# One of forty loads moved to another queue: the second load issued by ScalarE while SP issues the first

## The chip, the cores and the metric

The kernel runs on one core of one Trainium2 chip. The metric is device time in microseconds (us); lower is better. The time before is 627.82 us, the median of three runs (627.81 to 627.84). The profile is one further execution of the same program, with a span of 625.8 us.

On this core, VectorE (DVE in the profile) does nearly all of the arithmetic, ScalarE (ACT) and GpSimd (POOL) help at the very end, and SyncE (SP) issues the loads. An instruction that issues a transfer takes a fraction of a microsecond on its engine. The transfer itself then runs on 16 DMA engines, and a semaphore tells the waiting engine that it has landed.

## The reference

The input `x` is 8192 x 8192 in float32, 268 MB. The output is the infinity norm of each row, that is, the largest absolute value in it:

```python
def reference(x):
    return np.linalg.norm(x, ord=np.inf, axis=1)
```

Every element is read from memory once and takes part in one comparison.

## The kernel before

The 8192 rows are laid over 128 partitions, 64 rows in each: a first group of 46 rows per partition, then one of 18. A load of the main part, `(16384, ())` below, brings two rows of every partition (128 x 16384 floats, 8.39 MB, 64 KB in a row for each partition). There are 30 of those and one more of the same size, then one of half that size, and then six small ones. All but the last small load go into one ring that holds three of the large loads.

```python
GROUPS = [46, 18]
WHOLE = (
    [(16384, ())] * 30 + [(16384, (3712, 3680)), (8192, (2016, 1984))]
)
LAST = [
    (3920, (1680,)), (1984, (848,)), (1040, (432,)), (576, (240,)), (320, ()), (352, ())
]
RING = 3 * 16384
```

Each load is issued by SP. It takes the next place in the ring. If that place is still in use, it has to wait for the reduce that reads the old contents; the framework adds this wait by itself. For half of the loads the kernel declares that no further wait on the earlier load into the same place is needed, because the reduce in between already orders the two.

```python
    def load(pos, w):
        # ... place in the ring: at, buf ...
        inst = nc.sync.dma_start(out=buf, in_=x_of[first[row]][:, a : a + w]).ins
        if pos + w < R * n_cols:
            if (len(loads) + 4) % 10 < 5:
                for b, v, earlier in loads:
                    if b < at + w and at < b + v:
                        tc.declare_no_dep(
                            inst, earlier, reason="ordered by the reduces in between",
                        )
            loads.append((at, w, inst))
        return buf
```

The main loop loads a piece and reduces it on VectorE, one result for each row:

```python
    for u, (w, g) in enumerate(WHOLE):
        buf = load(pos, w)
        row, k = pos // n_cols, w // n_cols
        pos += w
        whole = k - 1 if g else k
        if whole:
            red = absmax(
                res[:, row : row + whole],
                buf[:, : whole * n_cols].rearrange("p (c m) -> p c m", m=n_cols),
            )
        # ... the last two pieces are shared with ScalarE and GpSimd ...
        if u == 1:
            not_before(
                keep(nc.scalar.activation(res[:, :1], res[:, :1], ABS)),
                red, "not before the second row is in",
            )
```

The one activation in the loop, after the second reduce, is ScalarE's only work before the last pieces come in. Behind the main loop, small pieces are shared out among VectorE, ScalarE and GpSimd, so that little work is left when the last byte lands. ScalarE's queue and SP's then store the results (32 KB in all).

In what follows the loads are numbered from 0: load 0 and load 1 are the first two, and reduce n is the reduce of load n. Load 3 takes the place of load 0 in the ring, load 4 that of load 1, and so on. The line numbers in the profile are those of the whole kernel: L108 issues a load, L68 is `absmax`, L140 is the activation in the loop, and L90 and L75 are the shares of ScalarE and GpSimd at the end.

Of the kernel before, what the change touches and what calls it, by code (L numbers as in the profile page):

```python
# [1 line left out]

# [4 lines left out]

P = 128
FP32 = mybir.dt.float32
INT32 = mybir.dt.int32  # L10
MAX = mybir.AluOpType.max
X = mybir.AxisListType.X
ABS = mybir.ActivationFunctionType.Abs
# [16 lines that stand above are left out]
@with_exitstack  # L30
def kernel(
    ctx: ExitStack,
    tc: tile.TileContext,
    x: bass.AP,
    out: bass.AP,
):
    nc = tc.nc
    n_rows, n_cols = x.shape
    R = n_rows // P
    assert R == sum(GROUPS) and n_cols == 8192  # L40
    keep = tc.keep_in_program_order


    first = []
    x_of, out_of = {}, {}
    for k in GROUPS:
        f = len(first)
        x_of[f] = x[f * P : (f + k) * P].rearrange("(p r) m -> p (r m)", r=k)
        out_of[f] = out[f * P : (f + k) * P].rearrange("(p r) -> p r", r=k)
        first += [f] * k  # L50

    single = ctx.enter_context(tc.tile_pool(name="single", bufs=1))

    ring = single.tile([P, RING], FP32)
    res = single.tile([P, R], FP32)

    n_parts = sum(1 + len(g) for w, g in LAST[:-1])
    last = single.tile([P, LAST[-1][0] + n_parts], FP32)

    def not_before(inst, other, why):  # L60
        tc.add_manual_dep(
            inst.ins, other.ins.name,
            mybir.DependencyInfo(mybir.DependencyClass.Sync, mybir.DependencyReason.DATA),
            reason=why,
        )

    def absmax(dst, src):
        return keep(nc.vector.tensor_reduce(  # L68
            out=dst, in_=src, axis=X, op=MAX, apply_absolute_value=True,
        ))  # L70

    def max_pool(dst, src):

        pool = nc.gpsimd
        keep(pool.add_instruction(  # L75
            mybir.InstTensorReduce(
                name=nc.get_next_instruction_name(),
                ins=[pool.lower_ap(src.bitcast(INT32))],
                outs=[pool.lower_ap(dst.bitcast(INT32))],
                op=MAX,  # L80
                axis=X,
            )
        ))

    def shared(part, buf, g):

        a = buf.shape[1] - sum(g)
        red = absmax(part[:, :1], buf[:, :a])
        for i, c in enumerate(g):
            keep(nc.scalar.activation(buf[:, a : a + c], buf[:, a : a + c], ABS))  # L90
            max_pool(part[:, 1 + i : 2 + i], buf[:, a : a + c])
            a += c
        return red

    loads = []

    def load(pos, w):

        row = pos // n_cols
        a = pos - first[row] * n_cols  # L100
        if pos + w == R * n_cols:
            buf = last[:, :w]
        else:
            at = loads[-1][0] + loads[-1][1] if loads else 0
            if at + w > RING:
                at = 0
            buf = ring[:, at : at + w]
        inst = nc.sync.dma_start(out=buf, in_=x_of[first[row]][:, a : a + w]).ins  # L108
        if pos + w < R * n_cols:
            if (len(loads) + 4) % 10 < 5:  # L110

# [10 lines that stand above are left out]
    pos = 0  # L122
# [10 lines that stand above are left out]
        if g:  # L133
            part = single.tile([P, 1 + len(g)], FP32, name=f"part{u}")
            shared(part, buf[:, whole * n_cols :], g)
            max_pool(res[:, row + whole : row + k], part)
# [8 lines that stand above are left out]
    n = LAST[-1][0]  # L145
    for h, (w, g) in enumerate(LAST[:-1]):
        buf = load(pos, w)
        pos += w
        shared(last[:, n : n + 1 + len(g)], buf, g)
        n += 1 + len(g)  # L150

    load(pos, LAST[-1][0])
    absmax(res[:, R - 1 :], last)
    final = nc.sync.dma_start(out=out_of[first[-1]][:, GROUPS[-1] - 1 :], in_=res[:, R - 1 :])


    for f, o in out_of.items():
        k = min(o.shape[1], R - 1 - f)
        early = keep(nc.scalar.dma_start(out=o[:, :k], in_=res[:, f : f + k]))
    tc.add_manual_dep(  # L160
        early.ins, final.ins.name,
        mybir.DependencyInfo(mybir.DependencyClass.NoSync, mybir.DependencyReason.SCHED_ONLY),
        reason="takes the later semaphore",
    )


# [1 line left out]
_INS = ['x']  # L168
_OUTS = [((8192,), 'float32')]


# [23 lines left out]
```

## Time and profile before

| what | value |
|---|---|
| time, median of three runs | 627.82 us |
| span of the profiled execution | 625.8 us |
| VectorE busy | 536.5 us (86%) |
| ScalarE busy | 15.0 us (2%) |
| GpSimd busy | 14.1 us (2%) |
| read from memory | 268.44 MB, 429 GB/s over the span |
| VectorE idle, waiting for loads | 86.7 us in 31 waits, the first of them 22.7 us |

Each row of the profile's table of groups names a source line, an engine and an operation, and then output and input with their shapes. Behind the bar come the busy time and the mean time of one in nanoseconds, and then the idle time of the engine just before such an instruction with its releaser (what ended the wait). The chain of waits follows the work that ended last back to the beginning. A busy share is an average over the span; whether an engine sets the end is read from the chain and from the waits.

### The profile page before, as it was taken

The numbers are of one execution on the slowest core, as the hardware profiler recorded it, in microseconds if no ns is written. First come the engines' busy times: TensorE is split into PE (matmuls) and PEld (weight loads), VectorE is DVE, ScalarE is ACT, GpSimd is POOL, SyncE is SP. The second block draws the span as 40 slices with busy tenths as digits, with TensorE's granted clock in tenths as the row PEclk, the third lists the DMA queues.
The fourth block names the chain that finished last, engine by engine and source line by source line (L and its number), as shares of the span: only waits on it lengthen the run. The fifth ranks groups of instructions, "written<-read, shape, count | busy, mean of one in ns | idle before, by whom it ended". The sixth has DMA issues, their size and how long they took to land.

```text
span 625.8 us, 173 instructions
## 1 busy us (share of the span) xinstructions
DVE 536.5 (86%) x39; ACT 15.0 (2%) x10; POOL 14.1 (2%) x14
## 2 busy tenths in 40 slices
DVE  0588988889888899888898888988889888899888
ACT  0000000000000000000000000000000000000044
POOL 0000000000000000000000000000000000000026
DMA  9999999999999999999999999999999999999997
GB/s 402 402 469 402 469 402 469 402 469 402 465 406 457 415 431 440 411 461 402 469 402 469 402 469 402 465 406 461 411 448 423 419 452 406 465 402 469 402 436 304
DMA packets 5904, 268.47 MB, mean 429 GB/s; under 512 B 1040, under 2 KB 1296, under 8 KB 1680
## 3 DMA queue, kind: packets, MB, share of 16 engines
q1 hardware_dynamic: 5616, 268.44, 99.3%
q10 hardware_dynamic: 288, 0.03, 0.0%
HBM read 268.44 MB, written 0.03 MB: 429 GB/s over the span
## 4 chain that ended last, share of the span: by engine, by line
DMA 71%; DVE 28%; SPq 0%; issue 0%; DVEq 0%
DMA ring<-in_x_dram 71%; DVE res L68 28%; DVE last L68 1%; SPq L108 0%; DVEq L68 0%
## 5 line engine op out<-in xcount | busy, mean ns | idle before, releaser
L68 DVE TENSOR_REDUCE res<-ring 128x2 f32<-128x16384 f32 (+1 forms) x31 | 525.3, 16944 | 86.7 <-DMA ring<-in_x_dram 86.7
L90 ACT ACTIVATE ring<-ring 128x3712 f32<-128x3712 f32 (+7 forms) x8 | 13.6, 1718 | 549.3 <-DMA ring<-in_x_dram 549.2
L75 POOL TENSOR_REDUCE part<-ring 128x1 int32<-128x3712 int32 (+3 forms) x4 | 10.1, 2562 | 607.8 <-ACT ring L90 607.8
L68 DVE TENSOR_REDUCE part<-ring 128x1 f32<-128x800 f32 (+1 forms) x2 | 5.5, 2748 | 0.1
L68 DVE TENSOR_REDUCE last<-ring 128x1 f32<-128x2240 f32 (+4 forms) x5 | 5.3, 1115 | 0.1
L75 POOL TENSOR_REDUCE last<-ring 128x1 int32<-128x1680 int32 (+3 forms) x4 | 3.4, 855 | 0.5 <-ACT ring L90 0.4
L140 ACT ACTIVATE res<-res 128x1 f32<-128x1 f32 x1 | 0.2, 202 | 57.3 <-DVE res L68 57.3
L140 ACT ACT_TABLE_LOAD x1 | 1.3, 1283 | 0.7 <-PEq L179 0.7
L68 DVE TENSOR_REDUCE res<-last 128x1 f32<-128x361 f32 x1 | 0.5, 529 | 0.1
L75 POOL TENSOR_REDUCE res<-part 128x1 int32<-128x3 int32 x2 | 0.4, 198 | 0.1
L179 POOL MEMSET const-float32-0.0<- 128x1 f32 x1 | 0.1, 100 | 0.2 <-issue 0.2
L179 POOL MEMSET const-bfloat16-1.0<- 128x1 bf16 x1 | 0.1, 103 | 0.0
L179 POOL MEMSET const-uint8-127<- 128x1 uint8 x1 | 0.1, 102 | 0.0
L179 POOL MEMSET const-float32-1.0<- 128x1 f32 x1 | 0.1, 99 | 0.0
## 6 DMA issues: line engine op xcount, KB each, us to landing
ring<-in_x_dram SPq DMA_DIRECT2D x1, 4096.0 KB, 31.2
ring<-in_x_dram SPq DMA_DIRECT2D x1, 1960.0 KB, 35.4
ring<-in_x_dram SPq DMA_DIRECT2D x1, 992.0 KB, 37.4
ring<-in_x_dram SPq DMA_DIRECT2D x1, 520.0 KB, 38.2
ring<-in_x_dram SPq DMA_DIRECT2D x31, 40.8
ring<-in_x_dram SPq DMA_DIRECT2D x1, 288.0 KB, 38.4
last<-in_x_dram SPq DMA_DIRECT2D x1, 176.0 KB, 38.3
ring<-in_x_dram SPq DMA_DIRECT2D x1, 160.0 KB, 38.3
```

Source lines behind the costliest of these rows:

```text
L68: return keep(nc.vector.tensor_reduce(out=dst, in_=src, axis=X, op=MAX, apply_absolute_value=True,))
L75: keep(pool.add_instruction(mybir.InstTensorReduce(name=nc.get_next_instruction_name(), ins=[pool.lower_ap(src.bitcast(INT32))], outs=[poo ...
L90: keep(nc.scalar.activation(buf[:, a : a + c], buf[:, a : a + c], ABS))
L140: keep(nc.scalar.activation(res[:, :1], res[:, :1], ABS)),
L179: nc = _bacc.Bacc("TRN2", target_bir_lowering=False, num_devices=1)
```

## The change

The load with number 1 is issued by ScalarE's queue instead of SP's. At that time one load has been recorded, so `len(loads) == 1` holds for it alone. SP issues load 0 and then goes on to load 2 without load 1 between them. All other loads stay with SP. The purpose is to have the first two issue instructions run side by side on two engines instead of one after the other on SP.

```diff
@@ -105,7 +105,9 @@
             if at + w > RING:
                 at = 0
             buf = ring[:, at : at + w]
-        inst = nc.sync.dma_start(out=buf, in_=x_of[first[row]][:, a : a + w]).ins
+
+        queue = nc.scalar if len(loads) == 1 else nc.sync
+        inst = queue.dma_start(out=buf, in_=x_of[first[row]][:, a : a + w]).ins
         if pos + w < R * n_cols:
             if (len(loads) + 4) % 10 < 5:
```

The amount of data, its layout, the ring, the reduces and everything at the end are as before.

## The prediction

> **What bounds the kernel now.** I read the page's busy shares first, then the waits, then the chain, and last the start of the run in the timeline and in the trace's records of single DMA packets.
>
> ```profile
> DVE 536.5 (86%) x39; ACT 15.0 (2%) x10; POOL 14.1 (2%) x14
> ...
> DMA  9999999999999999999999999999999999999997
> ...
> q1 hardware_dynamic: 5616, 268.44, 99.3%
> ```
>
> No compute engine fills the span. The 16 DMA engines do: q1, the queue of SP's loads, has packets on them for 99.3% of it. What VectorE waits for, and what SP waits for:
>
> ```profile
> DVE res L68 <- DMA ring<-in_x_dram: 86.7, 31, 22.7
> ...
> SPq L108 <- DVE res L68: 526.2, 29, 19.0
> ```
>
> VectorE waits before each of its 31 large reduces, and always for a load. SP waits for reduces, because a place in the ring has to be free, but this wait costs nothing as long as the DMA engines still have an earlier load to work on. The start, from the timeline of VectorE:
>
> ```profile
> 22.75 17.22 DVE L68 TENSOR_REDUCE res<-ring 128x2 f32<-128x16384 f32 x1 [22.75 <-DMA ring<-in_x_dram]
> 42.10 17.22 DVE L68 TENSOR_REDUCE res<-ring 128x2 f32<-128x16384 f32 x1 [2.13 <-DMA ring<-in_x_dram]
> 61.45 17.22 DVE L68 TENSOR_REDUCE res<-ring 128x2 f32<-128x16384 f32 x1 [2.13 <-DMA ring<-in_x_dram]
> ```
>
> The loads come in every 19.35 us (42.10 - 22.75, 61.45 - 42.10). A reduce takes 17.22 us, so VectorE has 2.13 us to spare in each period. The chain of waits alternates between loads and reduces:
>
> ```profile
> 1.17 40.91 DMA ring<-in_x_dram
> 42.07 0.02 issue
> 42.10 17.23 DVE res L68
> 59.33 0.02 issue
> 59.34 40.77 DMA ring<-in_x_dram
> ```
>
> The 40.77 us from issue to landing is two loads of 19.35 us in a row: the issued load waits behind the one in front of it. The reduces in the chain are therefore not a limit of their own. In the packet records no DMA engine has a gap over 0.1 us between packets from the first load until 622 us. So the end is set by the stream of bytes, a start before it and a tail after it.
>
> **What the Trainium skill says.** "DMA: Bandwidth & Descriptors", section "Where 436 GB/s comes from", gives 435.2 GB/s as the ceiling of the 16 ports. The trace agrees: 8.39 MB in 19.35 us is 433.5 GB/s, 99.6% of it. The same page, section "Issuing engines are not separate DMA queues", says that transfers from SP and ScalarE run on the same 16 engines and interleave, and that issuing from both saves only sequencer time. Its section "Queues, rings and completion order" says that each DMA engine takes turns between the queues that have work, one packet at a time. The trace of the kernel before has only one queue with loads, so neither statement is shown by it.
>
> **The change part by part.**
>
> *Issue time.* In the trace SP issues load 0 at 0.74 us, load 1 at 1.17 and load 2 at 1.64; an issue takes 0.38 to 0.43 us. The change lets load 1 go about 0.43 us earlier (if ScalarE issues it before its 1.28 us table load, which starts at 0.73; otherwise 0.9 us later, at about 2.0) and load 2 about 0.47 us earlier. But load 0 alone keeps all 16 DMA engines busy from 1.74 us (its first packet) to 22.37 us (the end of its last). The gain of the earlier issue is hidden behind it: 0 us.
>
> *Order of the packets.* A load is 128 packets of 64 KB, 8 for each DMA engine; a packet takes 2.42 us, the very first of each engine about 3.1 us. Now load 0 and load 1 share the engines in turn. Both together are 16 packets per engine and end where load 1 ended before, at about 42.1 us as VectorE sees it. Load 0 has the last packet but one on each engine, so it lands one packet earlier: 42.1 - 2.4 = 39.7 us. If the engines interleave more finely than a whole packet, load 0 lands close to 42.
>
> *VectorE.* Reduce 0 starts at 39.7 instead of 22.75 us, 17.0 later. Reduces 0, 1, 2 then run without a pause, each 17.24 us with the gap: they end at 56.9, 74.2, 91.4. The reduces stay behind by 17.0 us at first and catch up 19.35 - 17.24 = 2.11 us for each load, so after 8 to 9 loads (about 200 us) VectorE is again waiting for data and the run is as before. Of the 31 large reduces more than 20 remain then. The wasted idle time of VectorE at the start costs nothing at the end.
>
> *Does the stream break?* Load 3 needs the place of load 0, so it is issued when reduce 0 ends: 56.9 us instead of 40.0. From issue to first packet the trace shows 1.0 us at the start (0.74 to 1.74). So it could begin at 57.9. The DMA engines need it when load 2 runs out: in the trace before, the first packets of load 3 begin at 60.4 us. The margin is 60.4 - 57.9 = 2.5 us. For each later load it grows by 2.11 us. In the less favourable case that load 0 lands at 42.1, reduce 0 ends at 59.3, and load 3 can begin at 60.3: the margin is 0.1 us, and some engines may run dry for a few tenths and begin with a slow first packet (0.7 us more than 2.42). I allow up to 1 us for this once, and give it a weight of one in three: +0.2 us.
>
> *Rate of the stream.* At 99.6% of the ceiling named above a better interleaving can bring at most 0.4%, and only over the 40 us in which both queues have work: 0.15 us. Taking turns may cost as much. I set it to 0. The packets before take 2418 ns (median) in the first six or seven loads and 2422 ns later; if another order of starts kept the lower figure for all the rest, 24 loads x 8 packets x 4 ns = 0.8 us would be won. I see no reason why it should persist, and count 0.1 us.
>
> *Sum.* 627.8 + 0 (issue) + 0 (reduces) + 0.2 (risk of a short gap) - 0.1 (packet time) = 627.9 us.
>
> **The rivals.**
>
> *The stream breaks.* If ScalarE's queue were starved while SP's has work, load 0 and load 2 would land first, at 22.75 and 42.1 us, and load 3, issued at 40, would follow at once on SP's queue. Load 1 would then land only at about 80.8. Its reduce would end at 98.0, and load 4, which takes its place, could not be issued before that: the DMA engines would stand idle from about 80 to 99, some 18 us, and the time would be about 646 us. Nothing in the trace of before speaks for or against it; the page that describes taking turns speaks against it. I give it 3%.
>
> *The start gets better.* If the slow first packets (3.1 against 2.42 us) come from a lone queue filling its pipeline, two queues could hide that. It would bring at most 0.7 us: 627.1. Against it speaks that all 16 engines begin within half a microsecond of each other, with two further loads queued behind, and the second packet of each is already at 2.42 us.
>
> *A wait in SP's order.* The changed load has a semaphore that ScalarE's queue raises. Before, SP waited for DMA 14 times, 43.4 us in total, for loads whose data had been needed by a reduce first. A wait of this kind on load 1 before load 4 ends at 42 us in either kernel, long before load 4 is due; it makes 0 us.
>
> **Range and chances.** The sum is bounded from below by the stream: about 619.5 us of full packets (32 loads' worth at 19.36), which no order of queues shortens, so more than 1 us of gain is hard to see. Above, the gap at load 3 is the only plausible loss, about 1 us, or a little more if two queues slow each other. That gives 627.1 to 629.0 for 8 times in 10. Faster than 2% would need 12.6 us, which is not there to be had: 1%. Slower by 2% is the starved queue or something unknown like it: 4%. The rest, 95%, is within 2%.
>
> **What would show it.** In the changed profile VectorE's first wait should be about 40 us instead of 22.75, and its total wait should stay near 86.7 us, because the idle time is moved from many waits of 2.13 us into one. Reduces 0 to about 8 should have no wait in front of them, and from load 9 on the waits of 2.13 us should be back at the same times as before. Load 3 should be issued at about 57 us, and the DMA row should stay at 9 throughout. ScalarE's queue should appear with one more transfer. I am wrong if the first reduce still starts near 22.75 us (no sharing), if the DMA row shows a hole near 60 or 80 us, or if the landings stop coming every 19.35 us while two queues are at work.

## The result and the profile after

The changed kernel takes 630.0 us (median of six runs, 629.17 to 631.1), the kernel before 627.83 us beside it (six runs, 627.44 to 627.98). The ratio is 1.0037 with a 95% interval of 1.0024 to 1.0049. The change costs some 2 us, a third of a percent. The prediction had 627.9 us and a range up to 629.0; the measured time lies above it.

From the page of the changed kernel, its busy shares, two of the rows of 40 slices and its queues:

```profile
DVE 535.8 (85%) x39; ACT 15.0 (2%) x10; POOL 14.1 (2%) x14
...
DVE  0039999999998898888998888988889888899888
...
DMA  9999999999999999999999999999999999999996
...
q1 hardware_dynamic: 5472, 260.05, 96.0%
q10 hardware_dynamic: 432, 8.42, 3.1%
```

ScalarE's queue is q10, with one load of 8.39 MB (of the program's 38 loads) more than before. VectorE begins two slices in, then has nine slices with 9 (90% busy or more), then its old rhythm. The row of the DMA engines shows no hole: each digit is a mean of 16 engines over 15.7 us, too coarse for what happened.

The timeline of the changed kernel, in two stretches (start, length, instruction, idle time before it):

```profile
0.73 0.40 ACTq L110 DMA_DIRECT2D ring<-in_x_dram  x1
0.74 127.23 SPq L110 DMA_DIRECT2D ring<-in_x_dram  x7
...
41.88 102.85 DVE L68 TENSOR_REDUCE res<-ring 128x2 f32<-128x16384 f32 x6 [41.88 <-DMA ring<-in_x_dram]
```

```profile
179.45 17.22 DVE L68 TENSOR_REDUCE res<-ring 128x2 f32<-128x16384 f32 x1 [0.47 <-DMA ring<-in_x_dram]
198.80 17.22 DVE L68 TENSOR_REDUCE res<-ring 128x2 f32<-128x16384 f32 x1 [2.13 <-DMA ring<-in_x_dram]
```

Both issues go out together, before ScalarE's table load. Reduce 0 starts at 41.88 us instead of 22.75. Eight reduces run without a pause, and reduce 9 is back in the old rhythm with 2.13 us of waiting. But in the kernel before, reduce 9 started at 196.90 us:

```profile
196.90 17.22 DVE L68 TENSOR_REDUCE res<-ring 128x2 f32<-128x16384 f32 x1 [2.13 <-DMA ring<-in_x_dram]
```

The 1.90 us between 196.90 and 198.80 is the whole difference of the two spans (627.7 - 625.8), so it arose before reduce 9 and is never made up. VectorE's own waits say little about where: they grow from 86.7 to 89.2 us in total.

```profile
DVE res L68 <- DMA ring<-in_x_dram: 89.2, 24, 41.9
```

The place is seen in the records of single DMA packets. These name no DMA engine; a packet is matched with the one that ended just before it, so the length of a single gap is an estimate. Load 3 was issued at 59.13 us, when reduce 0 was done. The first packets of load 3 on the 16 engines, in nanoseconds from the start of the span, before and after:

```
before  60397 60454 60482 60486 60515 60556 60568 60611 60624 60642 60668 60748 60749 60847 60855 61021
after   60530 60534 60592 60652 60679 60725 60726 60764 60837 61076 61145 61203 61378 61461 61666 61872
```

Load 2 runs out on the engines from 60.34 us on. In the kernel before, load 3 follows without a gap. In the changed one engines run dry: with this matching seven of them for more than 0.2 us and the worst for 1.53 us. The last engine to begin was idle for at least 1.0 us however the packets are matched, since all 16 had finished load 2 by 60.86 us. The first packets also take longer, 2.66 to 3.59 us on all 16 engines instead of 2.42. The last engine therefore begins its second packet of load 3 at 65.46 us, where the last one of the kernel before did so at 63.44, and with a queue that is full again this delay of 2.0 us stays. Until the end a load is complete only when that engine is: the 16 completions of load 2 (the semaphore events, one for each engine) lie 0.43 us apart, those of load 3 1.89 us (80.83 to 82.72), and those of load 9 still 1.85. In the kernel before they lie about 0.63 us apart throughout. The last bytes of input arrive at 624.38 us instead of 622.45.

Three theories were open. A: load 3 is issued too late, DMA engines run dry, and the slowest keeps its delay. B: two queues that take turns cost time, or spread the engines, by themselves. C: with another order of semaphores SP waits where it did not wait before.

### The profile page after: what moved, and what is told of

It reads as the page before. It is cut to its first block, busy times and chain, and to the rows that moved or that the text cites. A ratio compares the mean times of both kernels' runs of the same rounds, so it can differ in the third digit from the quotient of the medians.

```text
span 627.7 us, 173 instructions
## 1 busy us (share of the span) xinstructions
DVE 535.8 (85%) x39; ACT 15.0 (2%) x10; POOL 14.1 (2%) x14
## 4 chain that ended last, share of the span: by engine, by line
DMA 57%; DVE 42%; issue 0%; SPq 0%; DVEq 0%
DMA ring<-in_x_dram 57%; DVE res L68 41%; DVE last L68 1%; SPq L110 0%; DVEq L68 0%
## 5 line engine op out<-in xcount | busy, mean ns | idle before, releaser
L68 DVE TENSOR_REDUCE res<-ring 128x2 f32<-128x16384 f32 (+1 forms) x31 | 524.6, 16942 | 89.2 <-DMA ring<-in_x_dram 89.2
```

Source lines behind the costliest of these rows:

```text
L68: return keep(nc.vector.tensor_reduce(out=dst, in_=src, axis=X, op=MAX, apply_absolute_value=True,))
```

## The experiments

In each group the kernels ran on one chip beside the kernel before, which took 627.49 us (23 runs) in the first, 627.47 (41 runs) in the second and 627.49 (14 runs) in the third.

### The changed kernel again

> The changed kernel once more, beside the next three on the same chip. Every theory: 629.2 to 631.1 us, as in its first six runs, about 2 us over the kernel before.

Measured: 629.24 us, ratio 1.0027 (1.0018 to 1.0036). Beside the third group it was run once more:

> The changed kernel beside the two others on the same chip: 628.7 to 630.9 us.

Measured: 629.06 us, ratio 1.0024 (1.0015 to 1.0034). The loss is real on three occasions, 1.6 to 2.2 us in the medians. It is not the same in each execution (628.57 to 631.1 us over all), while the kernel before stays within 0.7 us over all its runs.

### Free the place earlier, keep both queues

Reduce 0 covers the first row and only 64 columns of the second; the rest of that row is left out.

```diff
+            if u == 0:
+                absmax(res[:, 0:1], buf[:, :n_cols])
+                red = absmax(res[:, 1:2], buf[:, n_cols : n_cols + 64])
+            else:
                 red = absmax(...)          # as before
```

> The changed kernel, but the second row of load 0 is reduced over its first 64 columns only, so that reduce 0 takes about 8.9 us instead of 17.2 and load 3 is issued at about 51 us instead of 59.1. Theory A (load 3 is issued too late, DMA engines run dry, the slowest one keeps its delay): the gap is gone, 627.8 us, within 0.3 of the kernel before. Theory B (two queues taking turns on the DMA engines cost time or spread the engines by themselves): nothing changes, 629.2 to 631.1 us. Theory C (ScalarE's load changes the order of semaphores or the waits of SP later on): nothing changes either, 629.2 to 631.1.

Measured: 627.46 us, ratio 1.0000 (0.9992 to 1.0008). The two loads still take turns and reduce 0 still starts at 41.90 us, but load 3 is issued at 50.74. No engine has a gap, and the completions lie about 0.5 us apart throughout.

```profile
41.90 94.63 DVE L68 TENSOR_REDUCE res<-ring 128x1 f32<-128x8192 f32 x7 [41.90 <-DMA ring<-in_x_dram]
```

Theories B and C fall here: both queues and the same semaphores are there, and the loss is not.

### One queue, but load 3 issued as late

```diff
# the kernel before, behind reduce 0:
+            if u == 0:
+                absmax(scratch[:, 0:2], buf.rearrange("p (c m) -> p c m", m=n_cols))
+                absmax(scratch[:, 0:1], buf[:, :1560])
```

> The kernel before, with one queue for all loads, but with two extra reduces of load 0 into a scratch tile behind reduce 0 (a whole one, and one over 1560 columns), so that VectorE gives the place of load 0 free at about 59.0 us, as in the changed kernel. Theory A: the same loss without any load on ScalarE's queue, 629 to 631 us, with gaps on some DMA engines at 60 to 62 us and landings spread by 1.5 us or more afterwards. Theories B and C: 627.8 us, because VectorE has 2.1 us to spare in each period and makes up for the delay.

Measured: 629.65 us, ratio 1.0031 (1.0019 to 1.0043). VectorE's rows of the timeline of this kernel (its `absmax` is L69):

```profile
22.50 17.22 DVE L69 TENSOR_REDUCE res<-ring 128x2 f32<-128x16384 f32 x1 [22.50 <-DMA ring<-in_x_dram]
39.64 19.02 DVE L69 TENSOR_REDUCE scratch<-ring 128x2 f32<-128x16384 f32 x2
58.58 34.34 DVE L69 TENSOR_REDUCE res<-ring 128x2 f32<-128x16384 f32 x2
```

Load 0 lands early, as in the kernel before, and its place is kept until 58.66 us by extra work alone. Load 3 is issued at 58.69, its first packets start from 60.56 to 62.39, and the completions afterwards lie 2.2 us apart. The loss of the changed kernel is made with no load on ScalarE's queue at all.

### More delay

```diff
# the changed kernel, behind reduce 0:
+            if u == 0:
+                absmax(scratch[:, 0:1], buf[:, :4096])
```

> The changed kernel with one extra reduce of 4096 columns of load 0 into a scratch tile behind reduce 0, about 4.4 us, so that load 3 is issued at about 63.5 us. Theory A: every DMA engine is dry by then, and the whole delay goes into the time: 4.4 us more than the changed kernel, about 633.6 to 635.5 us. Theories B and C: 629.2 to 631.1 us, as VectorE makes up for 4.4 us in two or three periods.

Measured: 632.35 us, ratio 1.0077 (1.0064 to 1.0089): 3.1 us over the changed kernel on the same chip, not 4.4. The chain of waits in this kernel:

```profile
41.86 17.22 DVE res L69
59.08 4.33 DVE scratch L69
63.40 119.90 DVE res L69 x7
```

Load 3 was issued at 63.43 us, 4.24 later than in the changed kernel profiled beside it (the run above with 629.24 us in the median). But the last engine began at 65.28 instead of 61.41, only 3.87 later, and the last second packet at 67.91 instead of 64.36, only 3.55 later; the spans of these two executions differ by 3.5 us (630.3 against 626.8). The completions were 0.5 us apart afterwards. With every engine dry, all of them restart close together, 0.95 to 1.85 us after the issue. So the direction and most of the size are as theory A has them; the expectation added the delay to a loss that already held the unequal restart of one engine.

### How early is early enough

The single-queue kernel with one whole extra reduce and nothing behind it; then with one of 14500 columns instead.

```diff
# late57                                             # late55
+  absmax(scratch[:, 0:2], buf.rearrange(...))       +  absmax(scratch[:, 0:1], buf[:, :14500])
```

> One queue as in the kernel before, one whole extra reduce of load 0 into a scratch tile, so that load 3 is issued at about 56.9 us: the moment that the prediction had for the changed kernel. If the time from issue to the first packet is at most the 1.0 us seen at the start (the prediction's figure), no DMA engine runs dry and the time is that of before, 627.5 us. If under load it is up to the 3.7 us seen when load 3 was issued at 58.7 us, the slowest engine is still late by about 0.2 to 0.4 us: 627.7 to 627.9 us, with a few gaps in the packet records near 60 us.

> The same with load 3 issued at about 55.0 us, some 5.4 us before the DMA engines need it. Both readings of the time from issue to first packet: 627.5 us, no gap.

Measured: 627.45 us for the first, ratio 1.0000 (0.9991 to 1.0008), and 627.43 us for the second, ratio 0.9999 (0.9991 to 1.0007). Neither has a gap. VectorE's rows of the first (L69 is again its `absmax`), in which the place of load 0 comes free at 56.91 us (39.70 + 17.21):

```profile
39.70 17.21 DVE L69 TENSOR_REDUCE scratch<-ring 128x2 f32<-128x16384 f32 x1
56.83 34.34 DVE L69 TENSOR_REDUCE res<-ring 128x2 f32<-128x16384 f32 x2
```

Issued at 56.94 us, 3.4 us before the first engine needs it, load 3 is in time; issued at 58.69, 1.6 us before, it costs 2.2 us. The prediction had the changed kernel issue load 3 at 56.9: had load 0 landed when it said, the change would, by this single-queue kernel, have cost nothing.

### Why load 0 lands so late

The prediction let load 0 land one packet before load 1. The packet records of the changed kernel, for what by its times is one DMA engine:

```
 start ns  took  queue  bytes
   36186   2418  SP     65536   last packet of load 0
   38600   2418  ACT    65536   last packet of load 1
   41014      9  SP         4   completion of load 0
   41020      9  ACT        4   completion of load 1
   41026   2418  SP     65536   first packet of load 2
```

The engine takes turns packet by packet, and the 4-byte write that reports the completion is recorded as a packet of its own. On this engine load 0's data is in at 38.60 us, but its completion lets the last 64 KB of load 1 pass. All 16 engines show this order; the last of them writes load 0's completion at 41.52 us, its semaphore event is at 41.86, and reduce 0 starts at 41.88. In the kernel before, with one queue, the completion of load 0 follows its own last packet within 10 ns. The next kernel tests it with another size: load 1 is split into two halves, and only the first, with packets of 32 KB, goes to ScalarE's queue.

```diff
-    [(16384, ())] * 30 + [(16384, (3712, 3680)), (8192, (2016, 1984))]
+    [(16384, ()), (8192, ()), (8192, ())] + [(16384, ())] * 28
+    + [(16384, (3712, 3680)), (8192, (2016, 1984))]
-            if (len(loads) + 4) % 10 < 5:
+            if (len(loads) + 3) % 10 < 5:
```

The 3 in place of the 4 keeps the declarations on the same later loads, since there is one load more. The kernel after this one has the same shift.

> The changed kernel, but load 1 is split into two halves of one row each, and only the first half goes to ScalarE's queue; its packets are 32 KB, about 1.21 us each. If load 0's completion waits for the other queue's last packet, reduce 0 starts at about 31.8 us; if it follows load 0's own last packet, at about 30.6. In either case load 3 is issued at about 49 us, well before 60.4, and theory A gives the time of before, 627.5 us, with ScalarE's queue still in use. Theories B and C: about 629 us.

Measured: 627.47 us, ratio 1.0000 (0.9992 to 1.0008), with no gap.

```profile
32.31 85.78 DVE L68 TENSOR_REDUCE res<-ring 128x2 f32<-128x16384 f32 x6 [32.31 <-DMA ring<-in_x_dram]
```

Load 0's last data packets end between 30.13 and 30.71 us, its completions are written between 31.34 and 31.92, each within 10 ns of the end of a 32 KB packet of the other queue. The wait shrank from 2.41 to 1.21 us, the length of the smaller packet. Whether the 4 bytes wait for their turn or are held back until the packet begun before them is done, these runs do not separate; either way they go out when that packet ends. Load 3 is then early enough, and the change costs nothing.

### The same change without the loss

The changed kernel with reduce 0 done row by row, and load 3 as two loads of one row, so that its first half needs only the first half of the place.

```diff
-    [(16384, ())] * 30 + [(16384, (3712, 3680)), (8192, (2016, 1984))]
+    [(16384, ())] * 3 + [(8192, ())] * 2 + [(16384, ())] * 26
+    + [(16384, (3712, 3680)), (8192, (2016, 1984))]
-            if (len(loads) + 4) % 10 < 5:
+            if (len(loads) + 3) % 10 < 5:
...
+            if u == 0:
+                absmax(res[:, 0:1], buf[:, :n_cols])
+                red = absmax(res[:, 1:2], buf[:, n_cols:])
+            else:
                 red = absmax(...)          # as before
```

> The changed kernel, but reduce 0 is done as two reduces of one row each and load 3 as two loads of one row each, so that the first half of load 3 can be issued at about 50.6 us, when the first half of its place is free. Theory A: 627.5 us, no gap. Theories B and C: about 629 us, as the changed kernel.

Measured: 627.47 us, ratio 1.0001 (0.9992 to 1.0009). This computes all that the changed kernel computes, keeps both queues, and has reduce 0 at 41.88 us as well. It is level with the kernel before, not better: the stream of bytes sets both.

### Away from the start

```diff
-        queue = nc.scalar if len(loads) == 1 else nc.sync
+        queue = nc.scalar if len(loads) == 10 else nc.sync
```

> Load 10 instead of load 1 goes to ScalarE's queue. If the loss has to do with the start of the program (both queues cold, slow first packets), there is none: 627.5 us. Theory A says that it does not: loads 9 and 10 take turns and land together at about 216 us, reduce 9 starts there instead of at 196.9, load 12 is issued at about 233.4 us, just as the DMA engines run dry (234.5), and the loss is that of the changed kernel, 1.2 to 3 us: 628.7 to 630.5 us.

Measured: 629.9 us, ratio 1.0038 (1.0026 to 1.0051). Its timeline:

```profile
175.41 0.38 ACTq L110 DMA_DIRECT2D ring<-in_x_dram  x1
...
216.21 51.47 DVE L68 TENSOR_REDUCE res<-ring 128x2 f32<-128x16384 f32 x3 [21.48 <-DMA ring<-in_x_dram]
```

Load 9 was issued 19 us earlier than load 10 but has to share the engines with it. Reduce 9 starts at 216.21 us instead of 196.90, load 12 is issued at 233.46, and engines run dry, by the same matching for up to 1.93 us. The loss does not need the start of the program.

### All odd loads on ScalarE's queue

```diff
-        queue = nc.scalar if len(loads) == 1 else nc.sync
+        queue = nc.scalar if len(loads) % 2 and w == 16384 else nc.sync
```

> All large loads with an odd number go to ScalarE's queue. Theory A: the loss at load 3 as in the changed kernel, and none later, because then each load is issued while some 10 us of the one before it are left: 628.7 to 630.5 us. Theory B (taking turns costs by itself): some 2 us for each pair of loads, 640 us or more.

Measured: 636.03 us, ratio 1.0139 (1.0123 to 1.0154), which neither theory had. In the order that the framework made of this kernel, SP also issued the very last small load at the start. The packet records show gaps at load 3 only, up to 0.98 us, and none later; the last bytes arrive at 623.41 us, 1.0 later than in the kernel before. So taking turns all through the run does not slow the stream. The other 7.5 us or so are at the end, as VectorE's rows of the timeline show (the first line is that of reduce 29 in the kernel before, the rest are of this one):

```profile
583.91 17.22 DVE L68 TENSOR_REDUCE res<-ring 128x2 f32<-128x16384 f32 x1 [2.13 <-DMA ring<-in_x_dram]
...
594.96 25.81 DVE L68 TENSOR_REDUCE res<-ring 128x2 f32<-128x16384 f32 x2 [2.14 <-DMA ring<-in_x_dram]
620.69 5.40 DVE L68 TENSOR_REDUCE part<-ring 128x1 f32<-128x800 f32 x2
626.01 5.21 DVE L68 TENSOR_REDUCE last<-ring 128x1 f32<-128x2240 f32 x5
631.34 0.53 DVE L68 TENSOR_REDUCE res<-last 128x1 f32<-128x361 f32 x1
```

Reduce 29 starts at 594.96 us instead of 583.91, because load 29 shared the engines with load 30. Reduce 8 was already that late (188.59 us instead of 177.56): here every load shares the engines with the next, and the delay stays. As long as the stream goes on it costs nothing, but at the end VectorE has that much work left: from 594.96 us on it has no pause over 0.2 us. Theory A was incomplete in that it counted lost DMA time only.

## Why the prediction was wrong

*The bound.* Right. The stream of bytes sets the time, and in each kernel but the last the added time is what the slowest DMA engine lost: 1.93 us at the last byte in the two profiles, 1.9 us in the spans. The other profiles agree. In the two repeats of the changed kernel, the single-queue kernel with the late issue and the one with more delay, the last engine's second packet of load 3 starts 0.93, 1.93, 2.18 and 4.48 us later than in the kernel before, and the last bytes arrive 0.97, 1.84, 2.10 and 4.48 us later.

*The issue time.* Right: 0.43 us earlier, and worth nothing.

*The order of the packets.* Here the prediction failed. It was right that whole packets take turns and that load 0 has the last packet but one. It took the end of load 0's data for its landing: 39.7 us. The completion goes out only behind the last packet of load 1, and reduce 0 began at 41.88. The prediction did name a landing near 42, but for another cause (interleaving more finely than a packet), which the records rule out.

*VectorE.* Right: back to its old waits at reduce 9, as worked out. But it is not back at the old times: reduce 9 starts 1.90 us later than before.

*Does the stream break?* The margin of 2.5 us at load 3 rested on the 39.7. With the measured landing load 3 was issued at 59.13 us, 1.2 us before the first engine ran out. The prediction's figure for the unfavourable case was too small as well. It took 1.0 us from issue to first packet, which is what the earliest engine needed at the start. In the changed kernel the slowest engine needed 2.74 us (59.13 to 61.87), and in the single-queue kernel with the late issue 3.70 (58.69 to 62.39), although all engines had finished load 2 by 60.86 and 60.79 us. And it counted the gap as "a few tenths", with a weight of one in three, +0.2 us; the loss is that of the slowest engine, 1.6 to 2.2 us in the medians, and it occurs in every run. The sign that it named for a broken stream, a hole in the DMA row near 60 us, did not appear, since the row is too coarse for a gap of 1.5 us. Of the two errors the landing decided: with the issue at 56.94 us in the single-queue kernel no engine began late and nothing was lost.

*Rate of the stream.* The packets do keep 2.418 us longer (to about 260 us instead of 120). What this is worth alone no run shows; it did not outweigh the gap.

*The rivals.* ScalarE's queue was not starved. The first packets were as slow as before, 2.9 to 3.3 us on 15 of the 16 engines. A wait in SP's order played no part: the two complete kernels with ScalarE's queue in use and load 3 in time are level with the kernel before.

## What to carry to other kernels

With a ring of few places, a load that is issued beside another one makes the older of the two land later, and so delays the reuse of its place: ask when the next load that needs this place can be issued, and how long before the DMA engines run out. Here 3.4 us were enough and 1.6 were not, and one such miss is kept to the end by the slowest engine, even though the compute engine had slack in every period. A second queue is no gain where the issue already hides behind a running transfer; and where loads share the engines near the end, the backlog of the compute engine has no time left to be made up.

## What the runs showed of the hardware that was not expected

- The completion write of a load is recorded as a packet of 4 bytes. With two queues at work it went out only after the other queue's packet: 2.41 us later behind one of 64 KB, 1.21 us behind one of 32 KB.
- The time from issue to first packet depends on what the DMA engines are doing. At the start it was 1.0 to 1.5 us over the 16 engines of the kernel before (2.1 us on one engine of the changed one), with all of them dry 0.95 to 1.85 us, but up to 2.74 and 3.70 us where the issue fell 1.2 to 1.6 us before they began to run out. Why it is longer there was not settled.
- A DMA engine that starts a load late stays late by the same amount as long as its queue never runs dry. The distance between the first and the last completion of each load (0.63 against 1.85 us for load 9) shows such an event hundreds of microseconds afterwards, while the row of mean DMA shares shows nothing. It shows only unequal delays: in the kernel with more delay, which lost 4.9 us, the completions were 0.5 us apart.
